# Joint 256-column attention scores, and small f32 products issued in turn into the two column halves of the PE array

## The chip, the cores and the metric

The kernel runs on one core of one Trainium2 chip. The metric is the device time of one execution in microseconds (us), and lower is better. A core has five engines that run side by side, each through its own list of instructions in a fixed order, and wait for one another with semaphores: PE (TensorE, matrix products), DVE (VectorE), ACT (ScalarE), POOL (GpSimd) and SP (SyncE, which here issues most of the DMAs). The profile keeps PE's loading of weights apart as PEld.

## The reference, cut to what matters

One inference step of a trunk with two layers: sliding-window attention with sinks, then RWKV-7 time mixing, for a prompt of 16 + 2048 tokens and for 8 sequences of 4 new tokens. Two places of it matter here. In the attention, each block of 128 queries sees the block of 128 keys before it and its own:

```python
kc = with_prev(blocks(k))          # 256 keys: the block before, and this one
vc = with_prev(blocks(v))
valid = (rel >= 0) & (rel < WINDOW) & (kpos >= 0)      # a window of 128
o = sink_attend(qb, kc, vc, rel_bias(table, rel), valid, sinks)
...
s = jnp.einsum('...qkgd,...skd->...kgqs', q, k) * (A_HEAD_DIM ** -0.5) + bias
p = jnp.exp(s - m)
o = jnp.einsum('...kgqs,...skd->...qkgd', (p / denom).astype(v.dtype), v)
```

There are 16 query heads in 4 groups of 4 (one group for each key/value head), with 64 elements in a head. In the time mixing, two of the six mixed inputs go through small factors of width 64, the first LoRA products:

```python
xmix = xn[None] + (xprev - xn)[None] * mu[:, None, None, :]
xw, xa = xmix[4], xmix[5]
z = (w0 + jnp.tanh(xw @ w1) @ w2)          # w1: 1024 x 64
a = jax.nn.sigmoid((a0 + (xa @ a1) @ a2))  # a1: 1024 x 64
```

## The kernel before, in words

The prompt is cut into tiles of 128 tokens (t = 1 to 16); tile 0 holds 32 rows for the meta tokens and the 32 sample tokens. Tiles are put in nine blocks: block 0 holds tiles 0 and 1 (192 columns), blocks 1 to 7 two tiles each (256 columns), block 8 tile 16 alone (128 columns). The kernel runs in three stages one after the other: the attention layer, the front of the time mixing (its code runs over blocks in `stage1` and `front`), and the rest (projections, recurrence in chunks of 32 tokens, output).

The dense projections are made with numbers split in two f16 parts, so each of them is three f16 products on PE: rows named `pd<-xp,wq` (queries), `pd<-xp,wk` (keys), `pd<-wv,xp` (values), `pd<-xp,wg` (gates), `pd<-w,yp` (the attention's output projection, in `residual`).

The attention of a tile is `attend`. It goes over two head groups `gi`, and within each over two halves. For one half (one key/value head, four query heads):

- Scores: f16 products of 128 queries with the 128 keys of this tile into the PSUM tile `sc`, and with the 128 keys of the tile before into `sp`; for each of the four heads, two parts each. The keys lie in `kp`, split and laid out so that a product contracts over all 128 rows; the keys before come from the `kp` of this block or of the block before (`kprev`).
- ACT copies `sc` to SBUF (`ssb`), DVE overwrites the part above the diagonal with `sp` (`copy_predicated`), POOL adds the bias, and `softmax` follows on DVE and ACT.
- PE transposes the result into `pt`, DVE splits it into `pc` (keys of this tile) and `pp` (keys before).
- Value products: `oT[hs] = vt . pc + vprev . pp`, two f32 products of 128 rows by 64 columns of weights with 512 moving columns. The half decides which 64 output partitions of `oT`, and so which 64 columns of the PE array, they use.

When both halves are done, DVE multiplies `oT` into the gates `gT`. The first LoRA products are in `front`: for each of the two inputs (`q`) and each of 8 chunks of 128 features, one f32 product of the mixed input `xm` (made by DVE in `mix`, two chunks to a tile) with `lw1`, into 64 partitions of `lps`; `q` decides which 64.

The profile shows an f32 product as two instructions ("passes"), an f16 product as one. A product with 64 columns of weights reads `128*64` in its row, one with all columns `128*128`.

The order in which each engine's instructions stand is not the order of the code. The kernel is built with a scheduler that places instructions by a model of their durations, so dense products of the next block stand between the steps of a tile's attention. `tc.issue_after(x)` holds an instruction behind `x` in that order. Pools with few buffers bind it further: one `pt`, one `oT`, three `ssb`, two `pc`, two `pp`, four `xm` in the second stage.

Of the kernel before, what the change touches and what calls it, by code (L numbers as in the profile page):

```python
# [10 lines left out]
F32 = mybir.dt.float32  # L11
# [8 lines left out]
P = 128  # L20
# [10 lines left out]
def tile_hybrid_step(ctx: ExitStack, tc: tile.TileContext, a, o, c):  # L31
# [211 lines left out]
    with ExitStack() as ph:  # L243
# [51 lines left out]

        def keys_values(b, x):

            nb = width[b]
            kf = wk.tile([P, 2, nb], F32, name="kf", tag="kf", bufs=2)

            kp = wk.tile([P, 2, 2, 2, nb], F16, name="kp", tag="kp", bufs=2)
            ps = pd.tile([P, 2, nb], F32, name="pd", tag="pd")
            for i in range(2):
                dense_ws(ps[:, i, :], w_k[i], x)
            act(kf, ps, scale=1.0 / WSC)
            for half in range(2):
                a_, b_ = HS[half][1], OS[half]
                act(kp[a_, 0, half], kf[a_])
                tt(v_, kp[a_, 1, half], kf[a_], kp[a_, 0, half], ALU.subtract)
                for part in range(2):  # L310
                    act(kp[b_, part, half], kp[a_, part, half])
# [78 lines left out]
        w_q = [load_block(ws, big, ("big", "xr")[i % 2], pair_cols(0, i), [KC, P], f"wq{i}", gain0, f"ws{4 + i}", late=i%2) for i in range(8)]  # L390
        front.append(keys_values(1, xb[1]))
        w_g = [load_block(ws, big, ("big", "xr")[i % 2], pair_cols(1536, i), [KC, P], f"wg{i}", gain0, f"ws{12 + i}", late=i%2) for i in range(8)]
# [46 lines left out]

        def attend(t, kpair, koff, kprev, poff, vt, vprev, qp, gT, off):  # L440
            for gi in range(2):
                oT = pa.tile([P, 4, P], F32, name="oT", tag="oT", bufs=1)
                for half in range(2):
                    kv, hs = gi * 2 + half, slice(half * 64, half * 64 + 64)
# [8 lines left out]
                    act(ss, sc)  # L453
                    v_.copy_predicated(out=ss, mask=upmask.unsqueeze(1).broadcast_to([P, 4, P]), data=sp)  # L454
                    tt(g_, ss, ss, bias[:, 4 * kv:4 * kv + 4, :], ALU.add)
                    if t == 1:
                        tt(v_, ss, ss, m1mask.unsqueeze(1).broadcast_to([P, 4, P]), ALU.add)
                    softmax(ss, P, 4, P, sinks[:, 4 * kv:4 * kv + 4])
                    pt = pa.tile([P, 4, P], F32, name="pt", tag="pt", bufs=1)
                    for g in range(4):  # L460
                        t_.transpose(out=pt[:, g, :], in_=ss[:, g, :], identity=ident)  # L461
                    pc = wk.tile([P, 4, P], F32, name="pc", tag="pc", bufs=2)
                    pp = wk.tile([P, 4, P], F32, name="pp", tag="pp", bufs=2)
                    tt(v_, pc, pt, cmask.unsqueeze(1).broadcast_to([P, 4, P]), ALU.mult)
                    tt(v_, pp, pt, pc, ALU.subtract)
                    mm(oT[hs], vt[:, kv * 64:kv * 64 + 64], pc, True, False)
                    mm(oT[hs], vprev[:, kv * 64:kv * 64 + 64], pp, False, True)
                gs = gT[:, 4 * gi:4 * gi + 4, off:off + P]
                tt(v_, gs, oT, gs, ALU.mult)
            store_y(t, gT[:, :, off:off + P])  # L470

        def meta_attend(y0):
            om = pa.tile([P, 8, 32], F32, name="oT", tag="oT", bufs=1)
            for kv in range(4):
# [10 lines left out]
                for g in range(4):  # L485
                    t_.transpose(out=pt[:32, g, :32], in_=sv[:, g, :], identity=ident[:32, :32])
                pT = wk.tile([P, 4, P], F32, name="pc", tag="pc", bufs=2)
                v_.tensor_copy(out=pT[:32, :, :32], in_=pt[:32, :, :32])
# [4 lines left out]
        def sample_attend(y0):  # L493
# [54 lines left out]
            yield  # L548
            os_ = pa.tile([P, 8, 32], F32, name="sp", tag="sp", bufs=2)
            for b in range(0, NB, 2):  # L550
# [21 lines left out]
        for b in range(nblk):  # L572
            if b < 2:
                (kf, kp, vts), qp = front[b], qps[b]
            else:
                kf, kp, vts = keys_values(b, xb[b])
# [18 lines left out]
            if b == 0:  # L595
# [6 lines left out]
                dma(vs0, v0[32:64])  # L602

                kprev = smp.tile([P, 2, 2, 2, P], F16, name="kprev0")
                g_.memset(kprev, 0.0)
                for part in range(2):
                    v_.tensor_copy(out=kprev[:, part, :, :, 112:128], in_=kp[:, part, :, :, 16:32])
# [3 lines left out]
                poff = 0  # L611
                meta_attend(y0)
# [12 lines left out]
            for t in blocks[b]:  # L625
                if t == 0:
                    continue
                off = place[t][1]
                attend(t, kp, off, kprev, poff, vts[t], vprev, qp, gT, off)
                kprev, poff, vprev = kp, off, vts[t]  # L630
            if b == late:
# [43 lines left out]
    nblk = len(blocks)  # L675
    XM = 4
    order = [min(1, nblk - 1), 0] + list(range(2, nblk))
# [39 lines left out]
    with ExitStack() as ph:  # L717
# [96 lines left out]
        def front(b, xn):  # L814
# [1034 lines left out]
```

## Time and profile before

| | us |
|---|---|
| Time before, median of 3 runs | 2667.41 (2664.33 to 2667.47) |
| The profiled execution, own time | 2663.1 |
| Its span, first to last instruction | 2661.1 |
| PE busy | 2443.7 (92%) |
| DVE busy | 1675.1 (63%) |
| ACT busy | 1220.2 (46%) |
| POOL busy | 1111.5 (42%) |
| Mean granted clock of PE | 0.971 |

The profiled execution is 2.0 us longer than its span, and 4.3 us below the median. Busy times are sums of modelled durations: products are pipelined, so where a product starts is known better than where it ends. In a row of the timeline "x16" tells how many like instructions were merged, and the two numbers ahead are the start of the first and the time to the end of the last; the time that a run of products keeps PE is read from its start to the start of the next row. In the tables by windows the five engines follow in the order of the heading, with the count of instructions in brackets.

### The profile page before, as it was taken

The numbers are of one execution on the slowest core, as the hardware profiler recorded it, in microseconds if no ns is written. First come the engines' busy times: TensorE is split into PE (matmuls) and PEld (weight loads), VectorE is DVE, ScalarE is ACT, GpSimd is POOL, SyncE is SP. The second block draws the span as 40 slices with busy tenths as digits, with TensorE's granted clock in tenths as the row PEclk, the third lists the DMA queues.
The fourth block names the chain that finished last, engine by engine and source line by source line (L and its number), as shares of the span: only waits on it lengthen the run. The fifth ranks groups of instructions, "written<-read, shape, count | busy, mean of one in ns | idle before, by whom it ended". The sixth has DMA issues, their size and how long they took to land.

```text
span 2661.1 us, 60331 instructions
## 1 busy us (share of the span) xinstructions
PE 2443.7 (92%) x24388; PEld 1646.4 (62%) x24388; DVE 1675.1 (63%) x3256; ACT 1220.2 (46%) x2992; POOL 1111.5 (42%) x1640
## 2 busy tenths in 40 slices
PE   6999999999999998899999998769898999899897
PEld 5867767767754444577776666455555555556563
DVE  7586564676655887866555655666566655656664
ACT  6675454565432333654334344444353544444332
POOL 4242121332111232633333325337676767766703
PEclk9999998999999999999999999889999999999899
DMA  8432212332246554422222224675454455454323
GB/s 201 126 106 94 73 56 76 128 103 64 90 124 205 179 196 158 140 88 90 100 89 92 90 84 141 158 204 120 116 140 102 122 133 127 113 129 122 83 59 82
DMA packets 346234, 312.94 MB, mean 118 GB/s; under 512 B 205546, under 2 KB 282218, under 8 KB 344131
## 3 DMA queue, kind: packets, MB, share of 16 engines
q1 hardware_dynamic: 344339, 305.30, 39.8%
q0 software_dynamic: 1616, 3.79, 0.6%
q8 instruction: 192, 3.15, 0.5%
q14 instruction: 87, 0.71, 0.1%
HBM read 191.15 MB, written 119.84 MB: 117 GB/s over the span
## 4 chain that ended last, share of the span: by engine, by line
PE 45%; POOL 20%; DVE 14%; DMA 9%; issue 5%; ACT 5%; SPq 2%; POOLq 0%; DVEq 0%; ACTq 0%
PE pd L38 29%; POOL X L44 7%; POOL XT L44 6%; PE oT L38 5%; DVE xm L47 3%; DMA LA<-la_d 3%; DVE xpr L44 2%; SPq L50 2%; PE pl L38 2%; POOL L L894 2%; PE po L38 2%; POOL var L44 2%; PE sp L38 1%; PE pt L461 1%; PE C L38 1%
## 5 line engine op out<-in xcount | busy, mean ns | idle before, releaser
L38 PEld LDWEIGHTS <-yp 128*128 128x128 f16 x1488 | 137.9, 98 | 171.8 <-issue 22.0
L47 DVE SCALAR_TENSOR_TENSOR xm<-dx,mu,xn 128x256 f32<-128x256 f32 (+2 forms) x432 | 206.7, 533 | 55.5 <-POOL dx L44 36.6
L44 POOL TENSOR_TENSOR ssb<-ssb,bias 128x512 f32<-128x512 f32 x64 | 86.1, 1352 | 307.7 <-DVE ssb L454 274.4
L44 POOL TENSOR_TENSOR X<-X,XT 128x126 f32<-128x126 f32 (+24 forms) x458 | 200.1, 437 | 33.0
L44 POOL TENSOR_TENSOR XT<-LA,X 128x126 f32<-128x126 f32 (+24 forms) x458 | 195.7, 427 | 33.4
L38 PE MATMUL pd<-wg,xg 128*128 128x512 f16 (+1 forms) x816 | 199.5, 390 | 0.0
L38 PE MATMUL pd<-xp,wq 128*128 128x256 f16 (+2 forms) x1728 | 189.2, 264 | 3.6 <-ACT qf L41 2.4
L38 PE MATMUL pd<-xp,wg 128*128 128x256 f16 (+2 forms) x1728 | 188.3, 269 | 0.2 <-DVE xp L44 0.2
L38 PE MATMUL pd<-wvv,xpr 128*128 128x512 f16 (+1 forms) x816 | 186.0, 385 | 0.0
L38 PE MATMUL pd<-xpr,w 128*128 128x256 f16 (+2 forms) x1728 | 185.5, 266 | 0.0
L38 PEld LDWEIGHTS <-wq 128*128 128x128 f16 x1728 | 155.0, 98 | 48.8 <-issue 33.5
L38 PE MATMUL po<-wo,yp 128*128 128x512 f16 x768 | 184.7, 383 | 0.6 <-DVE yp L47 0.6
L38 PE MATMUL pd<-xpr,wkk 128*128 128x256 f16 (+2 forms) x1728 | 181.2, 265 | 0.0
L38 PEld LDWEIGHTS <-wg 128*128 128x128 f16 x1728 | 160.2, 100 | 30.2 <-issue 11.7
L38 PEld LDWEIGHTS <-w 128*128 128x128 f16 x1728 | 156.1, 98 | 27.7 <-issue 11.6
L38 PEld LDWEIGHTS <-wkk 128*128 128x128 f16 x1728 | 159.0, 98 | 16.5 <-issue 0.4
L38 PE MATMUL pd<-w,yp 128*128 128x512 f16 x720 | 166.9, 380 | 1.7 <-DMA yp<-y 1.7
L44 DVE TENSOR_TENSOR Z<-C,pe 64x256 f32<-64x256 f32 x256 | 107.8, 421 | 63.2 <-PE C L38 57.8
L44 POOL TENSOR_TENSOR ps<-wst,ps 128x1024 f16<-128x1024 f32 x32 | 68.8, 2148 | 181.2 <-ACT wst L41 167.7
L38 PEld LDWEIGHTS <-xpr 128*128 128x128 f16 (+1 forms) x816 | 78.4, 100 | 100.6 <-issue 14.8
L44 DVE TENSOR_TENSOR L<-pz,smk 64x256 f32<-64x256 f32 x256 | 107.9, 421 | 47.9 <-ACT LAs L41 29.2
L44 DVE TENSOR_TENSOR xpr<-xm,xpr 128x512 f16<-128x512 f32 (+2 forms) x144 | 103.6, 737 | 43.4 <-ACT xpr L41 43.1
(360 smaller groups left out, 5141.5 us busy)
## 6 DMA issues: line engine op xcount, KB each, us to landing
wst<-in_rwkv_w_in SPq DMA_DIRECT2D x32, 512.0 KB
wsp<-ps SPq DMA_DIRECT2D x32, 512.0 KB
BK<-bk SPq DMA_DIRECT2D x32, 512.0 KB
L<-ar SPq DMA_DIRECT2D x64, 256.0 KB
x<-in_x_prompt SPq DMA_DIRECT2D x29, 512.0 KB
xn<-xn SPq DMA_DIRECT2D x14, 1028.0 KB
ar<-aro SPq DMA_DIRECT2D x28, 512.0 KB
bk<-bko SPq DMA_DIRECT2D x28, 512.0 KB
```

What stands on the lines that cost most here:

```text
L38: return t_.matmul(out=out, lhsT=lhsT, rhs=rhs, start=start, stop=stop, **kw).ins
L44: return e.tensor_tensor(out=out, in0=in0, in1=in1, op=op).ins
L47: v_.scalar_tensor_tensor(out=out, in0=in0, scalar=scalar, in1=in1, op0=op0, op1=op1)
L50: return nc.sync.dma_start(out=out, in_=in_).ins
L461: t_.transpose(out=pt[:, g, :], in_=ss[:, g, :], identity=ident)
L894: g_.memset(L[OS[e], e], 0.0)
```

## The change

Four things are changed.

- **Scores.** `kp` now holds 128 more key columns in front: those of the tile before the block. For blocks 1 to 8 DVE copies them from the `kp` of the block before; for block 0 they are cleared and the meta tokens' keys written there. One product then has 256 moving columns (keys before and keys of the tile) in place of two with 128, into one PSUM tile `sc` of twice the width. `sp` is gone.
- **Value products.** Both halves' `pc` and `pp` are made first (three buffers each in place of two), and the four products of a head group follow as a group, second half first and the halves in turn: `pp` of half 1, `pp` of half 0, `pc` of half 1, `pc` of half 0. An order edge holds the other three behind the first.
- **First LoRA products.** The mixed inputs of four chunks (two tiles for each `q`) are made first, and the eight products of these follow as a group, with `q` in turn; an order edge holds seven behind the first.
- **Buffers.** Eight `xm` in the second stage in place of four.

```diff
-            kp = wk.tile([P, 2, 2, 2, nb], F16, name="kp", tag="kp", bufs=2)
+            kp = wk.tile([P, 2, 2, 2, P + (nb if b else P)], F16, name="kp", tag="kp", bufs=2)
...
+            if b == 0:
+                g_.memset(kp[:, :, :, :, 0:112], 0.0)
             for half in range(2):
                 a_, b_ = HS[half][1], OS[half]
-                act(kp[a_, 0, half], kf[a_])
-                tt(v_, kp[a_, 1, half], kf[a_], kp[a_, 0, half], ALU.subtract)
+                for to, of in ((slice(112, P), slice(16, 32)), (slice(P, 2 * P), slice(64, 192))) if b == 0 else ((slice(P, P + nb), slice(0, nb)),):
+                    act(kp[a_, 0, half, :, to], kf[a_, :, of])
+                    tt(v_, kp[a_, 1, half, :, to], kf[a_, :, of], kp[a_, 0, half, :, to], ALU.subtract)
...
+            if b:
+                v_.tensor_copy(out=kp[:, :, :, :, 0:P], in_=prev[:, :, :, :, prev.shape[-1] - P:])
...
-                    sc = pa.tile([P, 4, P], F32, name="sc", tag="sc", bufs=2)
-                    sp = pa.tile([P, 4, P], F32, name="sp", tag="sp", bufs=2)
+                    sc = pa.tile([P, 4, 2 * P], F32, name="sc", tag="sc", bufs=2)
                     for g in range(4):
                         i = 4 * gi + g
-                        for ps, kk, ko in ((sc, kpair, koff), (sp, kprev, poff)):
-                            for part in range(2):
-                                mm(ps[:, g, :], qp[:, half, i, off:off + P], kk[:, part, half, gi, ko:ko + P], part == 0, part == 1)
+                        for part in range(2):
+                            mm(sc[:, g, :], qp[:, half, i, off:off + P], kpair[:, part, half, gi, koff - P:koff + P], part == 0, part == 1)
...
-                    mm(oT[hs], vt[:, kv * 64:kv * 64 + 64], pc, True, False)
-                    mm(oT[hs], vprev[:, kv * 64:kv * 64 + 64], pp, False, True)
+                    probs.append((pc, pp))
+                head = ExitStack()
+                for x, vals in ((1, vprev), (0, vt)):
+                    for half in (1, 0):
+                        kv = gi * 2 + half
+                        m = mm(oT[HS[half][1]], vals[:, kv * 64:kv * 64 + 64], probs[half][x], x == 1, x == 0)
+                        if (x, half) == (1, 1):
+                            head.enter_context(tc.issue_after(m))
+                head.close()
...
-    XM = 4
+    XM = 8
...
-            for q in range(2):
-                for qq in range(4):
-                    xm = mix(wk, 4 + q, qq, xn, dx, nb)
+            for qq in range(0, 4, 2):
+                xms = [[mix(wk, 4 + q, qq + x, xn, dx, nb) for q in range(2)] for x in range(2)]
+                head = ExitStack()
+                for x in (1, 0):
                     for u in range(2):
-                        kc = 2 * qq + u
-                        mm(lps[q * 64:q * 64 + 64, :nb], lw1[:, q, kc, :], xm[:, u, :], kc == 0, kc == KC - 1)
+                        kc = 2 * (qq + x) + u
+                        for q in (1, 0):
+                            m = mm(lps[q * 64:q * 64 + 64, :nb], lw1[:, q, kc, :], xms[x][q][:, u, :],
+                                   (qq, x, u) == (0, 1, 0), (qq, x, u) == (2, 0, 1))
+                            if (x, u, q) == (1, 0, 1):
+                                head.enter_context(tc.issue_after(m))
+                head.close()
```

The sample attention's output tile takes a buffer of `sc` in place of one of `sp`.

How this moves instructions is seen in PE's list. First the value products of one head group in the middle of the attention stage; rows `pd<-xp,wq` are dense products for queries of a later block, `pt` is the transpose. Before, a half's product with `pp` stands alone between dense products; its product with `pc` stands five dense products further up:

```order
L38 LDWEIGHTS wq_584
L38 MATMUL pd<-xp,wq_584 128x256
L38 MATMUL oT<-pp,vt 64x512
L461 MATMUL pt<-ident,ssb 128x128 x4
L38 LDWEIGHTS wq_584
L38 MATMUL pd<-xp,wq_584 128x256
```

In the changed list the four products of both halves stand in a row, with the next half's transposes right behind them:

```order
L38 LDWEIGHTS wq_582
L38 MATMUL pd<-xp,wq_582 128x256
L38 MATMUL oT<-pp,vt 64x512 x2
L38 MATMUL oT<-pc,vt 64x512 x2
L469 MATMUL pt<-ident,ssb 128x128 x4
L38 LDWEIGHTS wq_582
L38 MATMUL pd<-xp,wq_582 128x256
```

All 32 groups of the attention stand like this. Second, the first LoRA products of one block in the second stage on PE; rows `pd<-w,yp` are the dense output projection of the next tiles. Before, single products stand between dense ones:

```order
L38 MATMUL pl<-xm,lw_9972 64x256
L38 LDWEIGHTS yp
L38 MATMUL pd<-w_9531,yp 128x512
L38 MATMUL pl<-xm,lw_9972 64x256
L38 LDWEIGHTS yp
L38 MATMUL pd<-w_9533,yp 128x512
L38 MATMUL pl<-xm,lw_9972 64x256
```

Each product stands by itself there. Now all 16 of a block stand in one run (in six of the nine blocks; in the other three in two runs of eight):

```order
L38 LDWEIGHTS yp
L38 MATMUL pd<-w_9012,yp 128x512
L38 MATMUL pl<-xm,lw_9405 64x256 x16
L38 LDWEIGHTS yp
L38 MATMUL pd<-w_8998,yp 128x512
```

The 70 runs of these products have become 12. Third, DVE's list where the keys before are copied (`kp<-kp`), between the steps of an earlier block's attention, once for each block from the second on:

```order
L44 TENSOR_TENSOR ssb<-ssb,sm 128x512
L44 TENSOR_TENSOR pc<-pt,cmask 128x512
L319 COPY kp<-kp 128x8x128
L44 TENSOR_TENSOR pp<-pt,pc 128x512
L44 TENSOR_TENSOR sm<-sm,es 128x4
```

This row is new; in the list before, nothing stands in its place. Between the work of `pc` and `pp` there is one row more.

More of the change, by code (lines that the diff above doesn't have):

```diff
@@ L305, in keys_values @@
             act(kf, ps, scale=1.0 / WSC)
+            if b == 0:
+                g_.memset(kp[:, :, :, :, 0:112], 0.0)
             for half in range(2):
                 a_, b_ = HS[half][1], OS[half]
-                act(kp[a_, 0, half], kf[a_])
-                tt(v_, kp[a_, 1, half], kf[a_], kp[a_, 0, half], ALU.subtract)
+                for to, of in ((slice(112, P), slice(16, 32)), (slice(P, 2 * P), slice(64, 192))) if b == 0 else ((slice(P, P + nb), slice(0, nb)),):
+                    act(kp[a_, 0, half, :, to], kf[a_, :, of])
+                    tt(v_, kp[a_, 1, half, :, to], kf[a_, :, of], kp[a_, 0, half, :, to], ALU.subtract)
+                to = slice(112 if b == 0 else P, kp.shape[-1])
                 for part in range(2):
-                    act(kp[b_, part, half], kp[a_, part, half])
+                    act(kp[b_, part, half, :, to], kp[a_, part, half, :, to])
+            if b:
+                v_.tensor_copy(out=kp[:, :, :, :, 0:P], in_=prev[:, :, :, :, prev.shape[-1] - P:])
             vts = {}
@@ L390, in tile_hybrid_step @@
         w_q = [load_block(ws, big, ("big", "xr")[i % 2], pair_cols(0, i), [KC, P], f"wq{i}", gain0, f"ws{4 + i}", late=i%2) for i in range(8)]
-        front.append(keys_values(1, xb[1]))
+        front.append(keys_values(1, xb[1], front[0][1]))
         w_g = [load_block(ws, big, ("big", "xr")[i % 2], pair_cols(1536, i), [KC, P], f"wg{i}", gain0, f"ws{12 + i}", late=i%2) for i in range(8)]
@@ L438, in store_y, with attend @@
             (g_ if t == NT else nc.sync).dma_start(out=y0_d[t], in_=yp)
-        def attend(t, kpair, koff, kprev, poff, vt, vprev, qp, gT, off):
+        def attend(t, kpair, koff, vt, vprev, qp, gT, off):
             for gi in range(2):
                 oT = pa.tile([P, 4, P], F32, name="oT", tag="oT", bufs=1)
+                probs = []
                 for half in range(2):
-                    kv, hs = gi * 2 + half, slice(half * 64, half * 64 + 64)
-                    sc = pa.tile([P, 4, P], F32, name="sc", tag="sc", bufs=2)
-                    sp = pa.tile([P, 4, P], F32, name="sp", tag="sp", bufs=2)
+                    kv = gi * 2 + half
+                    sc = pa.tile([P, 4, 2 * P], F32, name="sc", tag="sc", bufs=2)
                     for g in range(4):
                         i = 4 * gi + g
-                        for ps, kk, ko in ((sc, kpair, koff), (sp, kprev, poff)):
-                            for part in range(2):
-                                mm(ps[:, g, :], qp[:, half, i, off:off + P], kk[:, part, half, gi, ko:ko + P], part == 0, part == 1)
+                        for part in range(2):
+                            mm(sc[:, g, :], qp[:, half, i, off:off + P], kpair[:, part, half, gi, koff - P:koff + P], part == 0, part == 1)
                     ss = wk.tile([P, 4, P], F32, name="ssb", tag="ssb", bufs=3)
-                    act(ss, sc)
-                    v_.copy_predicated(out=ss, mask=upmask.unsqueeze(1).broadcast_to([P, 4, P]), data=sp)
+                    act(ss, sc[:, :, P:2 * P])
+                    v_.copy_predicated(out=ss, mask=upmask.unsqueeze(1).broadcast_to([P, 4, P]), data=sc[:, :, 0:P])
                     tt(g_, ss, ss, bias[:, 4 * kv:4 * kv + 4, :], ALU.add)
@@ L575, in tile_hybrid_step @@
             else:
-                kf, kp, vts = keys_values(b, xb[b])
+                kf, kp, vts = keys_values(b, xb[b], kp)
                 rest = queries(b, xb[b])
@@ L602, in tile_hybrid_step @@
                 dma(vs0, v0[32:64])
[L604 to L607, printed above, removed]
                 vprev = smp.tile([P, 256], F32, name="vprev0")
@@ L628, in tile_hybrid_step @@
                 off = place[t][1]
-                attend(t, kp, off, kprev, poff, vts[t], vprev, qp, gT, off)
-                kprev, poff, vprev = kp, off, vts[t]
+                attend(t, kp, P + off if b else P, vts[t], vprev, qp, gT, off)
+                vprev = vts[t]
             if b == late:
```

12 lines of the change are left out of this document (6 added, 6 removed).

## The prediction

> **What bounds the kernel now.** I read the table by windows first, to see where the changed work lies; then the chain that ended last in those windows; then the rows of the changed products one by one. The changed products lie in two stretches, the attention stage (115 to 790 us) and the front of the time mixing (790 to 1062 us). The first two rows are the stretches (PE, PEld, DVE, ACT, POOL), the third is what lies behind them:
>
> ```profile
> 115.00:790.00 675.00, 661.02 (x5568) 475.58 (x5565) 431.88 (x875) 358.32 (x1016) 161.89 (x130) 0.98 0.28 91
> 790.00:1062.00 272.00, 258.14 (x1236) 125.56 (x1236) 201.32 (x391) 89.83 (x139) 68.80 (x53) 0.99 0.56 186
> 1062.00:2661.00 1599.00, 1433.15 (x16709) 965.57 (x16706) 972.77 (x1898) 698.74 (x1709) 839.63 (x1412) 0.96 0.42 114
> ```
>
> PE is busy for 98% of the first stretch and 95% of the second; DVE comes next with 64% and 74%. The chain of waits over the same two windows:
>
> ```profile
> by line: PE pd L38 50.9%; PE oT L38 18.1%; PE sp L38 5.1%; PE pt L461 4.9%; PE sc L38 3.4%; ACT ssb L41 2.6%; DMA wst<-in_rwkv_w_out 1.3%; DVE mx L44 0.9%; DVE ssb L44 0.9%; DVE gT L47 0.8%; PE pd L286 0.8%; DVE mx L418 0.8%; DVE xp L44 0.8
> by line: PE pd L38 28.3%; PE pl L38 18.3%; DVE xm L47 8.7%; DVE xpr L44 5.7%; issue 4.7%; DVE xlast L756 3.7%; PE pm L751 3.5%; DMA x<-in_x_prompt 3.5%; DVE xn L44 3.2%; DMA wst<-in_rwkv_w_in 3.0%; SPq L50 2.9%; DVE x L47 2.8%; ACT xs L41 2
> ```
>
> In the attention 18.1% of 675 us, 122 us, of the chain are value products (`oT`), and some 83% of it is PE: what PE is spared there is spared the stage, as long as the others keep up. In the second stretch the first LoRA products (`pl`) hold 18.3% of 272, 50 us, but PE in all only half of the chain; DVE's mixing and some DMAs hold much of the rest.
>
> **The value products, 128 of them** (16 tiles, 4 halves, 2 each). PE's timeline at two of them:
>
> ```profile
> 636.84 0.56 PE L38 MATMUL sc<-kp,qp 128*128 128x128 f16 x7
> 637.32 1.07 PE L38 MATMUL oT<-pc,vt 128*64 128x512 f32 x2
> 638.33 0.23 PE L38 MATMUL sc<-kp,qp 128*128 128x128 f16 x1
> ...
> 639.91 1.07 PE L38 MATMUL oT<-pp,vt 128*64 128x512 f32 x2
> 640.92 0.66 PE L461 MATMUL pt<-ident,ssb 128*128 128x128 f32 x4
> 641.41 0.28 PE L38 MATMUL sp<-kp,qp 128*128 128x128 f16 x2
> ...
> 115.00:790.00 675.00, 139.82 (x280) 26.29 (x280) 21.83 (x32) 0.98 0.28 91
> ```
>
> From the start of a product to the next row's is 1.01 us (638.33 - 637.32). Four f32 passes of 128 columns take 0.49 (641.41 - 640.92), about 0.11 each once the change of shape at the end is off; 512 columns are four times that, 0.44, two passes 0.88, and the remaining 0.13 is what an isolated product loses when PE changes over. (The last row is the whole stage for `oT` rows alone, as modelled durations.)
>
> What do passes cost that alternate between column halves? Before has such a run: the recurrence's scores (`pz`) alternate between output partitions 0 to 63 and 64 to 127, with 128 rows contracted and 64 columns of weights, as the value products have.
>
> ```profile
> 1946.31 1.05 PE L38 MATMUL pz<-L,BK 128*64 128x128 f32 x16
> 1947.19 0.64 PE L38 MATMUL C<-Z,LS 128*64 128x64 f32 x16
> ```
>
> Sixteen passes in 0.88 us, 0.055 each: half of the 0.11 above. Two passes in different halves run at the same time, and already the first pair does, since 8 pairs of 0.11 fill the whole 0.88. So a group of four products is 8 passes in 4 pairs: 4 x 0.44 + 0.13 = 1.89 us, against 4 x 1.01 = 4.04. Saved: 2.15 us a group, 32 groups, **69 us of PE**. From both sides: nothing overlaps, and only three changes of shape go (3 x 0.13 x 32 = 12 us); or the delay ahead of each isolated product counts too (the seven score products take 0.39 at the 0.056 each shown below, and `oT` starts 0.48 after them: 0.09 more, 3 x 0.09 x 32 = 9), 78 us. I take 69, since the `pz` row has the same shape of weights and rows and only fewer columns.
>
> Here a rule of the Trainium skill speaks against the change: "TensorE: Matmul & The Clock Gate", Part 3, The mechanism, says that a load of weights overlaps running products only when its group of rows differs; both halves here use all 128 rows. By it each load would wait, and the group would be near the 12 us end. The `pz` row shows the opposite (0.055 us a pass), so I give the rule a small chance, as the second rival.
>
> **The first LoRA products, 144 of them** (9 blocks, 16 each). One run of 14 passes, and one product between dense ones:
>
> ```profile
> 1030.64 3.21 PE L38 MATMUL pl<-xm,lw 128*64 128x256 f32 x14 [1.96 <-DVE xm L47]
> 1033.78 0.98 PE L751 MATMUL pm<-ident,xs 128*128 128x128 f32 x7
> ...
> 982.50 0.65 PE L38 MATMUL pl<-xm,lw 128*64 128x256 f32 x2
> 983.08 0.39 PE L38 MATMUL pd<-w,yp 128*128 128x512 f16 x1
> ...
> 790.00:1062.00 272.00, 73.28 (x288) 34.55 (x288) 6.46 (x18) 0.99 0.56 186
> ```
>
> A pass in a run is 3.14 / 14 = 0.224; a product alone is 0.58, again 0.13 over its two passes. All 288 passes kept PE for 73.28 us (the last row, of these products alone). After: 16 pairs a block. Seven blocks of 256 columns: 7 x 16 x 0.224 = 25.1; block 0 (192 columns) 2.7; block 8 (128) 1.8; twelve runs with a change of shape, 1.6: 31 us. Saved: **42 us of PE**; at the least, without overlap, the changes of shape alone: 70 runs become 12, 58 x 0.13 = 8.
>
> **The scores.** 1024 products of 128 columns become 512 of 256. Before, eight stand at 0.45 us; 65 dense ones of 256 columns give the new price:
>
> ```profile
> 609.32 0.61 PE L38 MATMUL sc<-kp,qp 128*128 128x128 f16 x8
> 609.77 0.61 PE L286 MATMUL pd<-ident,x 128*128 128x128 f32 x4
> ...
> 599.84 7.26 PE L38 MATMUL pd<-xp,wg 128*128 128x256 f16 x65
> 606.93 0.60 PE L286 MATMUL pd<-ident,x 128*128 128x128 f32 x4
> ```
>
> 1024 x 0.056 = 57 against 512 x 0.109 = 56: **1 us**. ACT's and DVE's reads of `sc` keep their sizes. The halved weight loads go beside products and give nothing; the cover is the products' own 0.109 us.
>
> **What is added.** Eight copies of 128 x 1024 f16 elements on DVE. No such copy stands before; the nearest are a copy of as many f32 elements (0.66 us), a tiny one, and the longest:
>
> ```profile
> L511 DVE COPY sS<-sT 128x1024 f32<-128x1024 f32 x1 | 0.7, 661 | 0.0
> 968.32 0.16 DVE L731 COPY xn<-xlast 128x8 f32<-128x8 f32 x1
> 963.28 3.58 DVE L756 COPY xlast<-xn 128x8 f32<-128x8 f32 x1
> ```
>
> Between 1 us (8 x 0.16) and 29 (8 x 3.58); I take 0.66, 5 us of DVE, hidden in the 243 us that DVE has free in the attention. Without that cover it costs these 5. The copy stands between the work of `pc` and `pp` and can hold up one group in each block. Block 0's two more copies on ACT and two more subtractions on DVE replace two small copies, in the first 115 us where PE mostly waits for weights; I take 0, between -1 and +2. No DMA is added or moved past another one's queue.
>
> **The new waits.** A group waits for `pp` of the second half, and on PE everything placed behind it waits too: the next transposes, and through them DVE's next `pc`. In the changed list 27 or more dense products of 0.109, 2.9 us, stand between that half's transposes and the group (in 30 of the 32 groups; in the other two nothing does, and PE waits there), and DVE's two steps for `pc` and `pp` are short:
>
> ```profile
> L44 DVE TENSOR_TENSOR pp<-pt,pc 128x512 f32<-128x512 f32 x64 | 43.9, 686 | 0.9
> L44 DVE TENSOR_TENSOR pc<-pt,cmask 128x512 f32<-128x512 f32 x64 | 43.8, 685 | 26.9 <-PE pt L461 26.6
> ```
>
> 1.37 us together, so the wait is covered while DVE is less than 1.5 us behind; the two bare groups lose some 1.4 us each, which is within the loss taken below. In the second stage DVE fills all eight `xm` before a run of 16 and gets buffers back only from it; its mixing for the next matrix queues behind that. Today DVE waits little for PE there (13.2 us of idle time before `xm`):
>
> ```profile
> L47 DVE SCALAR_TENSOR_TENSOR xm<-dx,mu,xn 128x256 f32<-128x256 f32 x184 | 84.1, 516 | 13.2 <-PE pl L38 13.2
> ```
>
> **What of it reaches the end.** PE is spared 69 + 42 + 1 = 112 us. What comes next is DVE. Two stretches in which tiles are attended, with their `oT` rows alone first (48 and 32 passes, so 12 halves and 8), then with all rows:
>
> ```profile
> 132.70:219.80 87.10, 25.74 (x48) 4.59 (x48) 4.26 (x7) 1.00 0.33 102
> 620.00:675.60 55.60, 17.16 (x32) 3.07 (x32) 2.46 (x4) 1.00 0.06 22
> ...
> 132.70:219.80 87.10, 86.88 (x666) 57.95 (x665) 69.31 (x143) 58.38 (x159) 31.65 (x24) 1.00 0.33 102
> 620.00:675.60 55.60, 55.14 (x398) 36.27 (x399) 36.18 (x77) 26.52 (x87) 7.75 (x8) 1.00 0.06 22
> ```
>
> In the first, DVE is busy 69.3 of 87.1 us, and 6 groups would bring it to 74.2, with DVE at 93%: in a fixed order it will not fill that, and I take 7 us of the 13. In the second, 4 groups bring 55.6 to 47.0 with DVE at 77%: mostly had; of the 56 us that the other 26 groups save I take 85%, 48. For the second stage 42 off 272 leaves 230 us, in which DVE's 201.3 are 88%, and half of the chain is not PE's; I take 27 of 42. Sum: 7 + 48 + 27 + 1 = **83 us**. 2663.1 - 83 = 2580 for a profiled execution; the median stands 4.3 higher than that one, so rounded down **2583 us**, 3.2% faster.
>
> **Rivals.**
>
> - PE bounds throughout, and all 112 us come: 2667 - 112 = 2555. For it: PE at 98% and 95%. Against: DVE at 93% in the first stretch.
> - Halves do not overlap, and only the changes of shape go: 12 + 8 + 1 = 21 us, 2646. Against: the `pz` row. The rule of the Trainium skill quoted above would have it so.
> - DVE takes over: the attention saves a half of 69 and the second stage nearly nothing, for want of `xm`: about 40 us, 2627. For it: DVE has 84 us in `xm` rows alone and PE's list places them late.
> - Slower: DVE falls behind in the attention, and each group waits for `pp` with the PE list behind it. It decides where a group waits 83 / 32 = 2.6 us on average; with one copy of 3.58 us ahead of each the groups would wait some 3.6 and the time be 2583 + 115 = 2698. Against: eight copies, not 32, and 1.5 us of cover.
> - The spared time is lost in other places of the list, since the scheduler also placed the third stage's rows anew: within 0.2% of 2667.
>
> **How the numbers follow.** 0.2% is about what a measurement of this kernel can tell from no change. The forecast 0.55 (2556 to 2612), PE throughout 0.15, DVE 0.17, no overlap 0.06, slower 0.04, no change 0.03. Faster: 0.93; same 0.03; slower 0.04. The range reaches from a little under the all-of-it case to a little over the DVE case, 2548 to 2632, and leaves out 0.13 and the edges.
>
> **What would show it.** Right: `oT` rows "x8", about 1.9 us from start to the next start; `pl` rows "x32" with 3.6 us; busy `oT` down from 139.82 to some 70 us; the attention near 620 us and the second stage near 245. Overlap is wrong if a group takes 3.6 us. The pass to the end is wrong if rows for `oT` or `pt` show idle time ended by DVE `pp` or `ssb`, or DVE's `xm` waits for `pl` beyond 13 us. The forecast is wrong as a whole if the stage behind 1062 us, in which nothing is changed but the places of some rows, is longer than its 1599 us by more than a few.

## The result, and the profile after

The changed kernel takes 2599.06 us (median of 4 runs, 2591.27 to 2605.2), the kernel before beside it 2665.87 us (2656.16 to 2667.47). The ratio is 0.9755, with a 95% interval of 0.9719 to 0.9791. The forecast was 2583 us. The profiled execution of the changed kernel takes 2605.2 us, with a span of 2603.1 and a mean granted clock of 0.962, and is thus the longest of the four.

The table by windows of the changed kernel, for the attention, the second stage and the rest (columns: us, then PE, PEld, DVE, ACT and POOL busy with the count of instructions, granted clock, DMA share, GB/s):

```profile
118.00:753.00 635.00, 591.59 (x5067) 466.66 (x5066) 431.30 (x883) 357.80 (x1016) 162.36 (x130) 0.97 0.30 97
753.00:1000.00 247.00, 219.93 (x1213) 113.78 (x1214) 196.35 (x387) 87.04 (x139) 80.89 (x53) 0.94 0.63 205
1000.00:2603.10 1603.10, 1442.07 (x16731) 969.87 (x16729) 968.84 (x1902) 699.74 (x1711) 838.61 (x1412) 0.96 0.42 113
```

PE's busy time in the attention went from 661 to 592 us, by 69. The stage itself became only 40 us shorter (675 to 635): PE was idle for 14 us of it before and is idle for 43 now. In the second stage 38 us of busy time and 25 us of length are gone, and the granted clock there fell from 0.99 to 0.94. The third row is as long as before to a few us (1599 then).

PE's timeline of the changed kernel at one group of value products, and at one run of first LoRA products:

```profile
151.28 1.08 PE L38 MATMUL oT<-pp,vprev 128*64 128x512 f32 x4
152.19 1.03 PE L38 MATMUL oT<-pc,vt 128*64 128x512 f32 x4
153.15 0.66 PE L469 MATMUL pt<-ident,ssb 128*128 128x128 f32 x4
...
853.03 3.67 PE L38 MATMUL pl<-xm,lw 128*64 128x256 f32 x32
856.64 1.69 PE L38 MATMUL pd<-w,yp 128*128 128x512 f16 x7
```

A group of eight passes takes 153.15 - 151.28 = 1.87 us to the next start, where four isolated products took 4.04. In the trace its passes start 7, 473, 7, 422, 7, 422, 7 and 523 ns apart: two at a time, one in each column half. The 32 passes of a LoRA run take 856.64 - 853.03 = 3.61 us.

The chain of waits, for the attention and then the second stage:

```profile
by line: PE pd L38 25.9%; ACT ssb L41 6.5%; PE sc L38 5.1%; DMA wst<-in_rwkv_w_in 4.5%; issue 4.3%; POOL ps L44 3.8%; PE oT L38 3.5%; SPq L50 3.2%; ACT ps L41 3.2%; DMA wst<-in_attn_w_out 2.6%; DVE yp L44 2.5%; ACT wst L41 2.3%; DVE mx L426
by line: DVE xm L47 22.2%; PE pd L38 11.1%; DMA x<-in_x_prompt 10.5%; issue 8.9%; DVE xpr L44 5.9%; DVE xn L44 5.9%; DVE x L47 5.8%; DVE xn L741 4.9%; SPq L50 4.6%; POOL ms L110 2.8%; DMA wst<-in_rwkv_w_in 2.5%; DVE lsp L44 2.2%; DMA yp<-y 
```

`oT` has fallen from 18.1% of the attention's chain to 3.5%, and `pl` no longer stands in the second stage's part that is shown (18.3% before). DVE's mixing, 8.7% before, now leads there with 22.2%.

**Where PE waits now.** Its waits in the attention, before (two rows) and after (four):

```profile
PE oT L38 <- DVE pc L44: 4.7, 3, 3.2
PE pd L286 <- DVE xp L44: 3.7, 5, 1.4
```

```profile
PE pd L38 <- DVE qp L47: 8.1, 6, 2.1
PE oT L38 <- DVE pp L44: 7.7, 6, 1.9
PE pd L286 <- DVE xp L44: 7.3, 5, 3.9
PE sc L38 <- DVE ssb L462: 4.5, 3, 2.4
```

The columns are us in total, times, and the longest. All four of the later rows name DVE, at four different places: it is late here and there with the queries' split, the probabilities, the inputs' split and the scores. In the second stage of the changed kernel:

```profile
PE pm L761 <- ACT xs L41: 11.8, 5, 3.5
PE pm L777 <- DVE lp L810: 7.0, 1, 7.0
PE pl L38 <- DVE xm L47: 6.2, 4, 3.5
```

**The account.** To see what became of the saved PE time I split each stage by PE's starts. The time from the start of a product to the next start is counted to the product; what goes beyond the product's own time (at the rate that runs of products show) by more than 0.3 us is a "long stall", and half of the rest is counted as "half clock" where the trace shows a granted clock of 0.5. There are two profiled executions of each kernel, the second from the last experiment. All in us:

| | length | value or LoRA products | scores | other products | long stalls | half clock |
|---|---|---|---|---|---|---|
| attention, before, first execution | 676.0 | 128.8 | 58.1 | 458.4 | 19.5 | 11.2 |
| attention, before, second execution | 666.8 | 129.3 | 58.2 | 458.7 | 19.2 | 1.5 |
| attention, after, first execution | 636.7 | 60.9 | 56.5 | 449.0 | 52.3 | 18.1 |
| attention, after, second execution | 629.6 | 59.7 | 56.5 | 448.8 | 52.8 | 11.8 |
| second stage, before, first execution | 268.1 | 66.6 | - | 185.4 | 13.5 | 2.6 |
| second stage, before, second execution | 268.5 | 66.6 | - | 185.6 | 14.1 | 2.1 |
| second stage, after, first execution | 245.3 | 30.1 | - | 178.7 | 27.1 | 9.4 |
| second stage, after, second execution | 242.8 | 30.1 | - | 179.0 | 26.5 | 7.2 |

By the means of the two executions, products in the attention cost 80 us less (values 69, scores 2, others 10), the stalls grew by 33 and the half clock by 9, so 38 came through. In the second stage products cost 43 us less (LoRA 36.5, others 7), stalls grew by 13 and the half clock by 6, and 24 came through. What stands ahead of the attention is 2 us longer and what lies behind the second stage 1 us shorter. So of 123 us that PE was spared, 62 reached the end.

### The profile page after: what moved, and what is told of

It is laid out like the page before. It is cut to its first block, busy times and chain, and to the rows that moved or that the text cites. A ratio compares the mean times of both kernels' runs of the same rounds, so it can differ in the third digit from the quotient of the medians.

```text
span 2603.1 us, 59317 instructions
## 1 busy us (share of the span) xinstructions
PE 2345.8 (90%) x23876; PEld 1630.3 (63%) x23876; DVE 1666.8 (64%) x3264; ACT 1218.3 (47%) x2994; POOL 1121.7 (43%) x1640
## 4 chain that ended last, share of the span: by engine, by line
PE 31%; POOL 21%; DVE 20%; DMA 11%; ACT 8%; issue 7%; SPq 3%; POOLq 0%; ACTq 0%; DVEq 0%
PE pd L38 22%; POOL X L44 6%; POOL XT L44 6%; DVE xm L47 5%; SPq L50 3%; DMA LA<-la_d 2%; DVE xpr L44 2%; PE po L38 2%; ACT ssb L41 2%; POOL var L44 2%; POOL L L911 2%; PE C L38 1%; DMA wst<-in_rwkv_w_in 1%; DMA x<-in_x_prompt 1%; PE sc L38 1%
## 5 line engine op out<-in xcount | busy, mean ns | idle before, releaser
L47 DVE SCALAR_TENSOR_TENSOR xm<-dx,mu,xn 128x256 f32<-128x256 f32 (+2 forms) x432 | 200.3, 523 | 48.3 <-POOL dx L44 47.1
L38 PEld LDWEIGHTS <-w 128*128 128x128 f16 x1728 | 157.7, 99 | 27.1 <-issue 9.7
```

Source lines behind the costliest of these rows:

```text
L38: return t_.matmul(out=out, lhsT=lhsT, rhs=rhs, start=start, stop=stop, **kw).ins
L47: v_.scalar_tensor_tensor(out=out, in0=in0, scalar=scalar, in1=in1, op0=op0, op1=op1)
```

## Experiments

The theory: the groups cost PE what the forecast said, and what is missing was lost because DVE is not ready in time. The rivals: the joint scores cost something beside the groups; the granted clock takes part of it; or part of the overlap isn't had. Ratios are to the kernel before, run on the same chip in turn.

**The parts alone.** Three kernels make one part each: the joint scores with their key copies; the grouped value products with three buffers; and the grouped LoRA products with eight `xm`.

```diff
 # scores_only: joint scores, with the products of before behind them
-                for x, vals in ((1, vprev), (0, vt)):
-                    for half in (1, 0):
...
+                    mm(oT[HS[half][1]], vt[:, kv * 64:kv * 64 + 64], pc, True, False)
+                    mm(oT[HS[half][1]], vprev[:, kv * 64:kv * 64 + 64], pp, False, True)
 # values_only: before, with the four value products grouped, 3 pc and 3 pp
 # lora_only: before, with the eight LoRA products grouped
-    XM = 4
+    XM = 8
```

> The kernel before with the joint 256-column scores alone (value products and LoRA products as before). Theory (PE pays for passes, and 512 products of 256 columns cost as much as 1024 of 128): within 8 us of before, the attention stage 675 us give or take 8. Rival (halving the number of products and weight loads is worth something of its own, or the copies of keys on DVE cost): a gain or a loss of 15 us or more.

> The kernel before with the grouped value products alone. Theory: this is nearly all that the attention stage gained, so 35 to 45 us under before, a group of four products 1.87 us, PE idle in the stage some 40 us. Rival (the joint scores carry part of it): less than 25 us under before.

> The kernel before with the grouped first LoRA products and eight xm buffers alone. Theory: parts add up, so 20 to 28 us under before, all of it in the second stage. Rival (the second stage gained only because the attention ended in another state): under 12.

| | median us | ratio | 95% interval | attention | second stage | rest |
|---|---|---|---|---|---|---|
| scores alone | 2656.48 | 0.9973 | 0.9956 to 0.9990 | 670.5 | 264.9 | 1606.6 |
| values alone | 2621.30 | 0.9839 | 0.9813 to 0.9865 | 625.6 | 268.5 | 1602.0 |
| LoRA alone | 2636.35 | 0.9894 | 0.9872 to 0.9917 | 672.4 | 243.5 | 1606.2 |

Each part acts in its own stage: the value products in the attention, LoRA in the second stage, where it gives the whole of what the changed kernel shows there. The scores are worth a small gain by themselves, 7 us by the ratio. The attention with the values alone is 11 us shorter than that of the whole change in its first execution (636.7), which called for the next kernel; the second execution of the changed kernel, taken later, has 629.6, so 7 of the 11 come and go between executions.

**Both groups without the joint scores.**

```diff
 # vals_lora: before + values_only + lora_only; sc and sp as before
+                head = ExitStack()
+                for x, vals in ((1, vprev), (0, vt)):
+                    for half in (1, 0):
...
-    XM = 4
+    XM = 8
```

> The kernel before with the grouped value products and the grouped LoRA products (eight buffers), with the scores as before (two products of 128 columns, sc and sp). Grouped values alone gave -45 us, grouped LoRA alone -28. Theory 1 (the joint scores cost some 11 us in the attention once the value products are grouped, because the attention with grouped values alone took 625.6 us and the changed kernel's 636.8): attention 622 to 629 us, second stage 243 to 247, total about 2666 - 45 - 28 = 2593 us, ratio to the changed kernel 0.996 to 0.999, to the kernel before about 0.973. Theory 2 (the 11 us are the placement that happened to be met, and the scores are worth their 5 to 8 us here too): attention 637 or more, total about 2606 us, ratio 0.978 or more.

Measured: 2602.13 us, ratio 0.9753 (0.9727 to 0.9779); attention 635.4, second stage 243.4, rest 1612.3, in a profiled execution that was the longest of its five (2609.29). My theory 1 fell: without the joint scores the attention is as long as with them. Nor is theory 2 right, since the median is that of the whole change. The account names the 10 us against the values alone: stalls 51.3 against 49.2, products 566.3 against 567.4, but half clock 17.8 against 9.0. So a cost of the joint scores shows in neither the stalls nor the products. The groups' ratios multiply to 0.9839 x 0.9894 = 0.9735, inside the interval; the scores, worth 0.27% alone, add nothing measurable to the groups.

**The same groups, not in turn.** The products stand together, but those of one half behind those of the other.

```diff
-                for x, vals in ((1, vprev), (0, vt)):
-                    for half in (1, 0):
+                for half in (1, 0):
+                    for x, vals in ((1, vprev), (0, vt)):
...
-                for x in (1, 0):
-                    for u in range(2):
-                        kc = 2 * (qq + x) + u
-                        for q in (1, 0):
+                for q in (1, 0):
+                    for x in (1, 0):
+                        for u in range(2):
+                            kc = 2 * (qq + x) + u
```

> The changed kernel with the same groups, but not in turn: in a value group both products of half 1 and then both of half 0, in a LoRA group four of one input and then four of the other. Theory (what pays is that passes in different column halves run at the same time): a value group costs 3.4 to 3.8 us in place of 1.87, a LoRA pass 0.21 in place of 0.11, and only the changes of shape stay gained: 5 to 30 us under before, 40 to 60 over the changed kernel. Rival (what pays is that the products stand together): as the changed kernel, within 10 us.

Measured: 2611.61 us, ratio 0.9801 (0.9777 to 0.9824): by the ratios some 12 us over the changed kernel, far from the 40 to 60 of my theory and just beyond the 10 of its rival. The attention takes 628.2 us, no longer than the changed kernel's, the second stage 250.4, the rest 1607.7. In this kernel's list for PE the order is `pp`, `pc` of one half, `pp`, `pc` of the other. PE's timeline shows another:

```profile
149.86 1.09 PE L38 MATMUL oT<-pp,vprev 128*64 128x512 f32 x4
150.77 1.03 PE L38 MATMUL oT<-pc,vt 128*64 128x512 f32 x4
151.73 0.66 PE L469 MATMUL pt<-ident,ssb 128*128 128x128 f32 x4
...
843.55 2.86 PE L38 MATMUL pl<-xm,lw 128*64 128x256 f32 x16 [1.42 <-DVE xm L47]
846.34 0.61 PE L38 MATMUL pd<-w,yp 128*128 128x512 f16 x2
```

The `pp` passes of the second half started beside those of the first, 13 ns behind them, ahead of the first half's `pc` passes, and the group takes 1.87 us again. I had expected 3.4 to 3.8; that was wrong. PE takes products of the other column half early when they stand close behind. It does not do so without limit: with four LoRA products of one half ahead of four of the other, 16 passes take 846.34 - 843.55 = 2.79 us, where the run in turn takes 3.61 / 2 = 1.80. All LoRA products cost 42.7 us at full clock against 30.1 in turn and 66.6 apart; these 13 us are about what the kernel is longer by. So turns matter in the long runs, and standing together is enough for four products.

**DVE relieved of `pp`.** `vt . pc + vprev . (pt - pc)` equals `(vt - vprev) . pc + vprev . pt`. ACT copies `pt`, POOL makes the difference once for each tile, and DVE's 64 subtractions for `pp` go.

```diff
+            dv = wk.tile([P, 256], F32, name="dv", tag="dv", bufs=2)
+            tt(g_, dv, vt, vprev, ALU.subtract)
...
-                    tt(v_, pp, pt, pc, ALU.subtract)
+                    act(pp, pt)
...
-                for x, vals in ((1, vprev), (0, vt)):
+                for x, vals in ((1, vprev), (0, dv)):
```

The same was done to the kernel before, and to the kernel with both groups and the old scores.

> The changed kernel with pp no longer made by DVE: ACT copies pt whole, and the second product of a half takes the weights vt - vprev (made once a tile by POOL), so that the sum is the same. Takes 64 x 0.69 = 44 us from DVE in the attention stage and gives 64 x 0.59 = 38 us to ACT. Theory (what PE is spared and the stage does not gain is waiting for a late DVE): the attention stage 12 to 30 us shorter than the 638 of the changed kernel, PE idle there down from 43 us to 15 to 30. Rival (the loss lies in the latency of a half's chain and in the fixed order, not in DVE's load): within 8 us of the changed kernel.

> The same edit on the kernel before. Theory (there PE is the bound and DVE has room): within 10 us of before, less than half of what the edit gives to the changed kernel. Rival (DVE was a bound already): as much as there, 12 us or more.

> As the one beside it, and the product weights of the keys before are taken against the whole pt, copied by ACT (pp), with the weights of this tile's keys as vt - vprev made by POOL: DVE loses 64 rows of 0.69 us, 44 us. In the changed kernel the same edit shortened the attention by 20 us and the total by 2 to 8. Theory 1 (DVE's lateness bounds the attention, and the joint scores cost 11): attention 603 to 612 us, total 2580 to 2590. Theory 2 (what the attention saves is given back behind it, by a lower granted clock and a later third stage): attention 603 to 617, but the stages behind longer by 7 to 12 us and the total within 5 us of the kernel beside it.

| | median us | ratio | 95% interval | attention | its stalls | second stage | rest |
|---|---|---|---|---|---|---|---|
| after, with it | 2597.18 | 0.9741 | 0.9717 to 0.9765 | 616.5 | 37.2 | 247.6 | 1609.8 |
| before, with it | 2665.18 | 0.9990 | 0.9978 to 1.0002 | 671.9 | 13.5 | 266.4 | 1607.3 |
| both groups and old scores, with it | 2591.79 | 0.9726 | 0.9708 to 0.9745 | 622.1 | 42.8 | 243.2 | 1608.8 |

The attention of the changed kernel with it, by windows and by PE's longest waits:

```profile
121.00:737.00 616.00, 583.74 (x5060) 464.16 (x5058) 390.08 (x818) 390.40 (x1078) 171.66 (x143) 0.98 0.32 102
```

```profile
PE pt L471 <- ACT pp L41: 5.0, 5, 1.5
PE pd L286 <- DVE xp L44: 3.2, 2, 1.9
PE sc L38 <- DVE ssb L464: 3.0, 1, 3.0
```

DVE is busy for 390 us in place of 431, PE's stalls shrink from 52 to 37, and the attention by 13 to 20 us against the two executions of the changed kernel. So 15 us of the stalls are tied to DVE's work on `pp`. In the kernel before, where PE bound the stage, the same relief takes 6 us of stalls (19 to 13.5) and nothing from the total that the interval can tell. Of the 33 us of stalls that the change added, then, 24 are added with the relief too (37.2 against 13.5): some 9 are shown to come from this work of DVE, and with the old scores the relief takes 9 us of stalls in all (51.3 to 42.8). That the rest of them are DVE's is read from the waits alone. The relief also takes one step out of the chain from `pt` to the products and places other rows anew; the runs do not tell these apart from the lighter load. And the total gains little: in the profiles 2 to 3 us of it go back ahead of the attention, 2 to 5 in the second stage and 7 behind it, there in stalls (183.8 against 176.5 and 179.3 in the rest). The last row has the lowest median of all kernels; its interval overlaps that of the changed kernel, so I don't call it better.

**Two small things of the second stage.** One kernel has DVE's two tiny copies for `xlast` on ACT; the other goes back to four `xm`.

```diff
 # after_tiny
-                v_.tensor_copy(out=xn[:, :, 0:1], in_=st_["xlast"])
+                act(xn[:, :, 0:1], st_["xlast"])
...
-                v_.tensor_copy(out=xl, in_=xn[:, :, nb:nb + 1])
+                act(xl, xn[:, :, nb:nb + 1])
 # xm4
-    XM = 8
+    XM = 4
```

> The changed kernel with the two copies of the last column (128 x 8 elements, xlast and xn) made by ACT in place of DVE. In the kernel before DVE spends 19.1 us on these 16 copies, up to 3.58 us each, in the second stage. Theory (in that stage too DVE is what PE waits for now): 4 to 15 us shorter. Rival (PE or DMAs hold the stage): within 4 us.

> The changed kernel with four xm buffers in the second stage, as before. Theory (a group needs four xm at once, so with four DVE can make none while a group runs or waits): the second stage 247 us becomes 255 to 270, 8 to 23 us over the changed kernel. Rival (the groups alone pay, the buffers do not matter): within 5 us.

The tiny copies: 2600.49 us, ratio 0.9741 (0.9719 to 0.9763); second stage 243.4, between the two executions of the changed kernel (245.3 and 242.8). They are not what holds DVE up, and what does hold up PE in the second stage is told by the waits above alone: none of the kernels here shortened it further.

Four buffers: 2630.25 us, ratio 0.9862 (0.9842 to 0.9883), so 1.1% is lost. The second stage is 252.1 us, 7 longer than in the first execution of the changed kernel, with 5.6 more of stalls. The larger part, 24 us, is behind it, in a stage whose code is the same. DVE's mixing rows there, with four buffers and then with eight:

```profile
L47 DVE SCALAR_TENSOR_TENSOR xm<-dx,mu,xn 128x256 f32<-128x256 f32 (+2 forms) x225 | 117.8, 576 | 41.4 <-POOL dx L44 38.0 <-PE pl L38 2.9
```

```profile
L47 DVE SCALAR_TENSOR_TENSOR xm<-dx,mu,xn 128x256 f32<-128x256 f32 (+2 forms) x200 | 110.0, 598 | 47.6 <-POOL dx L44 47.1
```

With four, 25 more mixing steps lie behind the start of the third stage, and a last wait for `pl` shows that LoRA products do too, one run of 32 passes. PE's stalls in the rest are 201.5 us against 176.5, which is the whole 24. About half of them stand at two places: PE's longest wait for a DMA there (`TT`) is 14.7 us against 8.9, and its waits for DVE's `Z` take 7.7 us against 0.7. Which of the rows that were placed anew brings them I did not follow up.

**Both kernels once more.**

> The changed kernel once more, for a second profile. In the first, half-clock windows cost the attention stage 18.8 us and the second stage 13.7 us against full clock, where grouped values alone had 10.2 and 3.4. Theory 1 (the windows belong to the program, because they follow PE's idle stretches of 1.5 us and more): the windows lie at the same places to some 5 us in at least two thirds of the cases, the loss in the attention is 15 to 22 us again and in the second stage 11 to 15. Theory 2 (the loss is that of one execution): the attention loses 8 to 13 us, and the stage is 626 to 631 us long. The median is 2593 to 2604 us in either case.

> The kernel before once more, for a second profile. Theory 1 (the half-clock windows belong to the program): the attention loses some 12 us against full clock and the second stage some 3 again (11.9 and 3.4 in the first profile), lengths 674 to 678 and 266 to 270 us. Theory 2 (the loss is that of one execution): the losses differ by 5 us or more from the first.

The changed kernel: 2598.32 us, ratio 0.9760 (0.9735 to 0.9785). The one run of the kernel before took 2659.73. The stalls repeat to 1 us in all four stages of the table; the half clock does not. Against full clock (its whole loss, with stalls that fall into it) the attention of the changed kernel lost 13.7 us and the second stage 11.9, where the first execution had 18.8 and 13.7; the kernel before 1.7 and 3.4, after 11.9 and 3.4. So neither theory is right as it stands, and there are two kinds of half clock. The first is tied to the program, behind PE's stalls. Outside 380 to 445 us, where the second kind lies, the attention of the kernel before lost 1.7 us in both executions and that of the changed kernel 8.5 and 10.2: this part came with the change. PE's timeline of the changed kernel, and the windows around it:

```profile
504.23 1.91 PE L38 MATMUL sc<-kp,qp 128*128 128x256 f16 x16
510.00 0.76 PE L286 MATMUL pd<-ident,x 128*128 128x128 f32 x4 [3.87 <-DVE xp L44]
```

```profile
494.00:510.40 16.40, 10.68 (x93) 8.90 (x92) 5.49 (x7) 8.36 (x13) 4.62 (x3) 1.00 0.41 130
510.40:513.80 3.40, 2.97 (x16) 1.97 (x15) 3.40 (x5) 1.23 (x3) 2.12 (x1) 0.50 0.51 159
513.80:554.00 40.20, 36.19 (x305) 29.04 (x303) 33.81 (x76) 32.67 (x98) 13.59 (x14) 1.00 0.30 92
```

PE waits 3.87 us for DVE, and the clock is 0.50 for the 3.4 us behind it. The second execution has the same stall with a half-clock window behind it. The second kind comes without a stall, between 380 and 445 us, and not the same in every execution. The kernel before at one place, in its first and its second execution:

```profile
405.40:436.00 30.60, 30.60 (x198) 24.00 (x196) 1.12 (x2) 6.14 (x13) 0.00 (x0) 0.67 0.12 35
```

```profile
405.40:436.00 30.60, 27.75 (x277) 23.87 (x276) 10.74 (x19) 11.20 (x28) 6.66 (x4) 1.00 0.31 93
```

In the first PE counts as busy throughout and has a clock of 0.67; in the second it has 1.00 there. The lengths of the attention (676.0 and 666.8) differ by 9 us, and the half clock cost 10. What this stretch has of its own are the products of the sample attention, whose output takes a buffer of `sp` in this kernel:

```profile
409.83 0.29 PE L38 MATMUL sp<-sT,vcs 128*64 128x16 f32 x2
410.05 0.28 PE L38 MATMUL sp<-sT,vs 32*64 32x16 f32 x2
```

Their passes have 16 moving columns and start 0.11 us apart, as far as dense passes of 256 columns (0.109), so PE reads as busy with a sixteenth of the columns. They come in four runs of 32 passes: in this execution at 401.5 to 404.9, 409.8 to 413.7, 419.6 to 423.2 and 429.4 to 432.8 us. The half clock sets in at 405.4, 412.2, 422.5 and 432.7. In all 14 profiles together 36 stretches of half clock begin between 380 and 443 us, and each begins inside such a run or at most 1.2 us behind one; at 20 of the 56 runs none begins, all four of the second execution of the kernel before among them.

## Why the prediction was right, and where it was off

- **The groups' prices were right.** The value group was forecast at 1.89 us and measured 1.87; a LoRA run at 3.6 and measured 3.61. In the account the value products cost 69 us less, as forecast. The `pz` row, with the same shape of weights and rows, was the right one to go by. The rule of the Trainium skill that was the second rival ("TensorE: Matmul & The Clock Gate", Part 3, The mechanism) does not hold for these products: both halves use all 128 rows, their passes start 7 ns apart, and the next loads of weights start 50 ns behind them, while they run.
- **PE was spared more than forecast**, 123 us for 112. The forecast had the delay of the rows ahead of isolated products as its upper end (9 us in the attention) and left it out. The account shows it: other products cost 10 us less in the attention and 7 in the second stage, and 9 and 6 us of that stand in the row directly ahead of a value or LoRA product. The upper end, 78 us, is what was had in the attention (69 + 10). LoRA's 42 came out near 43 by luck: the 73.28 us that it starts from are modelled durations, which run past the start of the next row. By starts the products kept PE for 66.6 us and now keep it for 30.1, which is 36.5; the other 7 are those of the other products, which the forecast did not count.
- **What of it reaches the end** is the step that was mis-sized. It took 55 of 69 us in the attention, where 38 of 80 came; in the second stage 27 of 42, where 24 of 43 came, which is near. The argument went by DVE's share of the stage (77% and 93%), and took two bare groups as the only places to wait. DVE's share did become no more than 431 / 635 = 68%, and PE waits for it all the same, in short waits at many places: a fixed order in which the saved engine arrives earlier at each thing it needs. The relief of DVE by 41 us showed that these waits are DVE's in part. The row that the forecast named for this, `oT` waiting for `pp`, is there with 7.7 us. Its other sign, DVE waiting for buffers of `xm`, did not come: 0.7 us of idle time before `xm` in the second stage of the changed kernel ended with `pl`.
- **The clock was not in the sum at all.** Each stall of some length can bring a stretch at half clock, so that idle time costs more than itself: 9 us in the attention and 6 in the second stage by the account.
- **The scores** were forecast at 1 us, gave 7 alone and nothing measurable beside the groups; PE's own price for them fell by 2.
- **The key copies** were taken at 0.66 us and measured a median of 0.42, with one of 1.75:

```profile
L319 DVE COPY kp<-kp x8: 410/418/1753, 33.8 to 625.0; 128x1024 f16<-128x1024 f16 x8
```

  Block 0's part, taken as 0 between -1 and +2, came out at its upper end: the time ahead of the attention grew by 2 us, in the kernel with the scores alone too (117.8 us against 115.9 and 115.5). The forecast took it that PE mostly waits for weights there. It does not: PE is busy for 91 of the first 115 us, and its longest wait, 5.6 us, is for the bias table.
- **The rest** was forecast to keep its 1599 us to a few. It does here (1601.2 and 1607.0 before, 1602.7 and 1602.6 after). Other kernels show that the risk was real: with four buffers it grew by 24 us, in the kernel with both groups and the old scores by some 10 (1612.3).

So by the profiles 62 us came through for a forecast of 83: 61 were lost in place of 29, and 11 more were spared. The two misses pull against each other, so the total is nearer than its parts. The medians are 67 us apart, and the changed kernel's stands 16 us from the forecast.

## What to carry to other kernels

Small products that use half of the array's columns should stand together, with the halves in turn where a run is long: a group of four costs less than half of what they cost apart, and the dense products beside them gain too. To forecast what a saving on the bounding engine is worth, do not go by the next engine's share alone. In a fixed order, count the places where the bounding engine now comes early, and add the half clock that may follow a stall; here half of the saving came through, though no other engine was busy for more than 80% of either stage.

## What the runs showed of the hardware that was not expected

- **Products of the other column half are started ahead of their place in the list**, where four stand together (passes 13 ns apart, group 1.87 us), and only in part where four of one half precede four of the other (2.79 us for 16 passes, not 1.80). The Trainium skill ("TensorE: Matmul & The Clock Gate", Part 3, The mechanism) says that products start strictly in the list's order; the records of this kernel show otherwise.
- **Half clock follows stalls much shorter than a window.** In the 14 profiles I took the stretch from 118 to 995 us without 380 to 445, where the other kind lies. Of 80 half-clock windows there, 79 begin within 6 us after a stall of 1.2 us or more; the windows are 3.4 us or a multiple of it. Seen from the stalls, 44 of 53 stalls of 3 us or more have one with them or behind them, 32 of 53 between 2 and 3 us, and 33 of 127 between 1.2 and 2. The Trainium skill ("TensorE: Matmul & The Clock Gate", Part 1, HAM oscillation — how this bites in real kernels) gives as its rule no idle gaps of PE beyond about 3.4 us; here shorter ones are often enough. The stalls of 1.2 us and more, with 6 us behind each, make up 16% of that stretch, so chance would not put 79 of 80 there. Still, that the stall brings the window is read from where they stand; no run changed the one without the other.
- **Half clock also comes without a stall, beside runs of products with 16 moving columns**: at 405 to 436 us it cost 10 us in one of two executions of the same kernel, and in 13 of the 14 profiles some of it stands between 380 and 443 us, each time in or right behind a run of 32 such passes. This too is read from where they stand; no run changed these products, and why the same runs bring none in another execution stays open.
